# A decoder layer's MLP: three 256-column matmuls per weight tile become one of 512 columns and one of 256

## The chip, the cores and the metric

The kernel runs on one core of a Trainium2 chip. The metric is the device time of one execution in microseconds (us). The time of the kernel before is the median of three runs; one further execution was taken with the hardware profiler, and all rows below come from it.

## What is computed

One decoder layer over 256 tokens of width 2048, all in float32: modulated RMSNorm, an input projection, two kinds of attention, an output projection with a gated residual, then modulated RMSNorm and an MLP, then a last RMSNorm. What the change touches is the MLP (hidden width 8192):

```
h = rmsnorm(x, mlp_norm_g) * (1.0 + sc2) + sh2
u = relu(h @ w_ff1)                  # 2048 -> 8192
x = x + g2 * ((u * u) @ w_ff2)       # 8192 -> 2048
```

`sc2`, `sh2`, `g2` are slices of `silu(c) @ w_mod + b_mod`.

## The kernel before

Activations stand transposed: 128 features on the partitions, the 256 tokens (`S`) as columns. A weight matrix is read from memory in pieces of 1 MB (128 x 2048) into a ring of buffers (`raw`), one DMA each, issued on SyncE's queue (SP).

**Split precision.** A large product isn't run on plain float32 tiles. `split` (L186) makes of each half of a weight piece (128 x 1024) a high part on ScalarE (ACT, L191, rounded to the type float32r) and a low part, the remainder, on VectorE (DVE, L192). Each has three buffers. The activations are split in the same way, into `h2h`/`h2l` and `uh`/`ul`. One tile of weights (128 x 128) times one tile of activations (128 x 256) is then three matmuls of 256 columns into the same 256 columns of a PSUM bank (`mm3`, L195): high weights by high activations (L196), high weights by low activations (L197), low weights by high activations (L198). I call these three a *step*. On the chip a matmul instruction has its own weight load, which the trace shows as the engine PEld beside PE. The matmuls of the stages before (input projection L262, attention) run on plain float32 tiles; the trace shows each of them as two matmuls.

**The MLP.** The hidden width is worked in 8 blocks of 1024, each of 8 tiles of 128. Blocks 0 and 1 are made first, in a loop over the 16 input tiles that holds all 8 PSUM banks (`pf`, L656 to L678). After that comes a loop, L746: `ff1(e)` makes block `e` (e from 2 to 7), `ff2(e - 2)` multiplies an earlier block into the 16 output tiles; `ff2(6)` and `ff2(7)` close.

- `ff1(e)` (L699): for each of 8 tiles `f`, one weight piece, 16 steps into the bank `pu`, then `u_out` (L649): on ACT relu out of PSUM (L651), square (L652), high part (L653); on DVE the low part (L654).
- `ff2(e)` (L716): for each pair of output tiles, one weight piece; for each output tile 8 steps into a bank `pd`, then one instruction that takes the bank's 256 columns: for e = 0 a copy on ACT into `y_sb`, for 1 to 5 an add on DVE (L734), for 6 and 7 a multiply-add into the residual `x_sb` (L739). In block 7 each output tile then goes into the sum of squares of the last RMSNorm.

The part of the modulation that gives `g2` is made during this loop: 16 pieces of `w_mod`, each reduced on DVE (L167), called by `pump_g2` at fixed places. A scheduler turns the program into one fixed order for each engine; every engine works its own list in order.

Earlier in the kernel, in the input projection, pieces of `w_mod` go through a ring of six buffers (`early_ring`, L150): two of the pool `rawp` and the four activation buffers `ah0`, `al0`, `ah1`, `al1`, which later hold the attention's output (`mixh`, `mixl`) and then `h2h`, `h2l`.

Of the kernel before, what the change touches and what calls it, by code (L numbers as in the profile page):

```python
# [46 lines left out]
WM = 3  # L47
G2F = (1, 5)
G2E = (3, 4, 5, 6)
G2E2 = (0, 1, 2, 3)  # L50
G2A = 6
LEADK = (1, 1)
PBN = 8

# [2 lines left out]
def kernel(  # L57
# [86 lines left out]
    def raw(name):  # L144
        return ring("w", name)
# [4 lines left out]
    def early_ring(name):  # L150
        n = early["n"] % 6
        early["n"] += 1
        if n < 2:
            return rawp.tile([P, 2048], F32, tag="rawm", name=name, bufs=NM)
        return actp.tile([P, 2048], F32, tag=("ah0", "al0", "ah1", "al1")[n - 2], name=name)

    def mod_col(part, i):

# [33 lines left out]
        V.tensor_tensor(out=lo, in0=src, in1=hi.bitcast(F32), op=ALU.subtract)  # L192
        return hi, lo

    def mm3(out, wh, wl, ah, al, start, stop, **kw):  # L195
        T.matmul(out, lhsT=wh, rhs=ah, start=start, stop=False, **kw)  # L196
        T.matmul(out, lhsT=wh, rhs=al, start=False, stop=False, **kw)  # L197
        T.matmul(out, lhsT=wl, rhs=ah, start=False, stop=stop, **kw)  # L198


    ap_stack = ExitStack()
# [75 lines left out]
        stage1_mm(kt, hs.pop(kt))  # L277
    nc.sync.dma_start(con, consts)
    g1 = []
    bias = [actp.tile([P, 8, S], F32, tag=f"a{g}1", name=f"bias{g}") for g in "hl"]  # L280
# [5 lines left out]
    mixh = [actp.tile([P, 8, S], F32R, tag="ah0", name="mixh0")]  # L286
# [180 lines left out]
    with tc.high_priority():  # L467
# [94 lines left out]
        units[0].rows()  # L562
        for n, u in enumerate(units):
            if n == 8:
                mixh.append(actp.tile([P, 8, S], F32R, tag="ah1", name="mixh1"))
                mixl.append(actp.tile([P, 8, S], F32R, tag="al1", name="mixl1"))
# [33 lines left out]
    for half in range(2):  # L600
        if half:
            ap_stack.close()
            wide_stack = ExitStack()
            wide.update(pool=wide_stack.enter_context(tc.tile_pool(name="wide", bufs=1)), w=WW, m=WM)
        for dp in range(8):
            w = raw(f"wo{half}_{dp}")
            nc.sync.dma_start(w, w_out[half, dp])
            for d2 in range(2):
                d = 2 * dp + d2
                wh, wl = split(w, d2, f"wo{half}_{dp}")  # L610
                pd = bank(f"pd{half}_{d}")
                for k in range(8):
                    o = k * P
                    mm3(pd[:, 0:S], wh[:, o : o + P], wl[:, o : o + P], mixh[half][:, k, :],
                        mixl[half][:, k, :], k == 0, k == 7)
# [8 lines left out]
        r2 = ss2.rstd()  # L624


    h2h_ = [actp.tile([P, 8, S], F32R, tag=f"ah{i}", name=f"h2h{i}") for i in range(2)]
    h2l_ = [actp.tile([P, 8, S], F32R, tag=f"al{i}", name=f"h2l{i}") for i in range(2)]
    h2h = [h2h_[kt // 8][:, kt % 8, :] for kt in range(KT)]
    h2l = [h2l_[kt // 8][:, kt % 8, :] for kt in range(KT)]  # L630

    def h2_tile(kt):
        a2 = small(f"a2_{kt}")
        V.tensor_tensor(out=a2, in0=sc2[kt], in1=vec[:, V_GM + kt : V_GM + kt + 1], op=ALU.mult)
        xn = tmp.tile([P, S], F32, tag="xn2", name=f"xn2_{kt}")
        if kt < 1:
            V.scalar_tensor_tensor(out=xn, in0=x_sb[:, kt, :], scalar=a2, in1=r2, op0=ALU.mult, op1=ALU.mult)
        else:
            G.tensor_scalar(out=xn, in0=x_sb[:, kt, :], scalar1=a2, scalar2=None, op0=ALU.mult)  # L639
            G.tensor_tensor(out=xn, in0=xn, in1=r2, op=ALU.mult)  # L640
        A.activation(out=h2h[kt], in_=xn, func=AF.Identity, bias=sh2[kt])  # L641
        V.scalar_tensor_tensor(out=h2l[kt], in0=xn, scalar=sh2[kt], in1=h2h[kt].bitcast(F32),
                               op0=ALU.add, op1=ALU.subtract)

    def new_u(e):
        return (up_pool.tile([P, 8, S], F32R, tag="uh", name=f"uh{e}"),
                up_pool.tile([P, 8, S], F32R, tag="ul", name=f"ul{e}"))

    def u_out(u, f, src):  # L649
        r = tmp.tile([P, S], F32, tag="relu", name="relu")  # L650
        A.activation(out=r, in_=src, func=AF.Relu)  # L651
        A.activation(out=r, in_=r, func=AF.Square)  # L652
        A.activation(out=u[0][:, f, :], in_=r, func=AF.Copy)  # L653
        V.tensor_tensor(out=u[1][:, f, :], in0=r, in1=u[0][:, f, :].bitcast(F32), op=ALU.subtract)  # L654

    pf = [bank(f"pf{b}") for b in range(8)]  # L656

# [1 line left out]
    for kt in range(KT):  # L659
# [56 lines left out]
    def ff2(e):  # L716
        uh, ul = us.pop(e)
        for dp in range(8):
            if e in G2E2 and dp in G2F:
                pump_g2(1)  # L720
            w = raw(f"wf2_{e}_{dp}")
            nc.sync.dma_start(w, w_ff2[e, dp])
            for d2 in range(2):
                d = 2 * dp + d2
                wh, wl = split(w, d2, f"wf2_{e}_{dp}")
                pd = bank(f"pd{e}_{d}")
                for k in range(8):
                    o = k * P
                    mm3(pd[:, 0:S], wh[:, o : o + P], wl[:, o : o + P], uh[:, k, :], ul[:, k, :], k == 0, k == 7)

                if e == 0:
                    A.activation(out=y_sb[:, d, :], in_=pd[:, 0:S], func=AF.Copy)
                elif e < G2A:
                    V.tensor_tensor(out=y_sb[:, d, :], in0=pd[:, 0:S], in1=y_sb[:, d, :], op=ALU.add)  # L734
                else:
                    if e == G2A:
                        V.scalar_tensor_tensor(out=x_sb[:, d, :], in0=y_sb[:, d, :], scalar=g2[d],
                                               in1=x_sb[:, d, :], op0=ALU.mult, op1=ALU.add)
                    V.scalar_tensor_tensor(out=x_sb[:, d, :], in0=pd[:, 0:S], scalar=g2[d], in1=x_sb[:, d, :],  # L739
                                           op0=ALU.mult, op1=ALU.add)  # L740
                if e == 7:
                    ss3.add(d)
                    A.activation(out=x_sb[:, d, :], in_=x_sb[:, d, :], func=AF.Copy,
                                 scale=vec[:, V_GF + d : V_GF + d + 1])

    for e in range(2, 8):  # L746
        ff1(e)
        ff2(e - 2)
    for e in (6, 7):
        ff2(e)  # L750
# [38 lines left out]
def _pack(inp):  # L789
# [62 lines left out]
```

## Time and profile before

| | |
|---|---|
| median of 3 runs | 1099.46 us (1096.85 to 1099.94) |
| profiled execution | 1097.01 us, of which the span from first to last instruction is 1095.2 us |
| mean granted TensorE clock | 0.987 of full speed |
| busy share of the span | PE 96%, PEld 90%, DVE 67%, ACT 44%, POOL 11% |
| bytes read | 275 MB, 253 GB/s over the span |
| chain that ended last | PE 84%, DVE 5%, DMA 4%, POOL 3% |

Matmuls overlap in the trace: one of 256 columns is shown as 283 ns long, while the next starts 120 ns after it. What a matmul costs in a stream is therefore read from starts, or from counts in a window, not from its length. In a table by windows the number in brackets counts every instruction that touches the window. SPq is SyncE's queue of DMA issues. A time in brackets at a row's end is idle time of the engine just before it, with what ended it.

### The profile page before, as it was taken

What the parts mean: (1) busy time and instruction counts of PE and PEld (TensorE: products, weight loads), DVE (VectorE), ACT (ScalarE), POOL (GpSimd) and SP (SyncE); (2) the same over time, 40 slices, a digit from 0 to 9 for tenths busy, and PEclk for the clock granted to TensorE, in tenths of its full rate; (3) what the DMA queues carried; (4) which work ended last, traced back from release to release, by engine and by line L of the source; (5) the groups of instructions that cost most, each with busy time, mean ns of one, the idle gap of its engine ahead of it and who ended that gap; (6) DMA issues with size and microseconds to landing.
All of it is one profiled execution on the core that took longest, in us unless ns stands there. A gap on an engine that the chain in (4) does not pass through costs nothing.

```text
span 1095.2 us, 18790 instructions
## 1 busy us (share of the span) xinstructions
PE 1047.9 (96%) x7860; PEld 990.0 (90%) x7860; DVE 733.8 (67%) x948; ACT 482.6 (44%) x788; POOL 115.4 (11%) x88
## 2 busy tenths in 40 slices
PE   5999999999977999999999999999999999999995
PEld 4777756689977999999999999999999999999995
DVE  6776478799986898887755555545554555676554
ACT  2000176643442435764553454355345345533362
POOL 1000012000337453000000000000000000000043
PEclk9999999999998999999999999999999999999997
DMA  8999976689996774888855555555455555554541
GB/s 345 427 427 426 415 277 231 224 313 402 426 426 233 281 280 181 308 338 324 326 209 188 193 180 174 186 193 182 170 188 192 183 171 186 192 185 169 186 155 77
DMA packets 42357, 278.43 MB, mean 254 GB/s; under 512 B 4832, under 2 KB 7456, under 8 KB 11424
## 3 DMA queue, kind: packets, MB, share of 16 engines
q1 hardware_dynamic: 42272, 277.23, 67.0%
q8 instruction: 61, 1.00, 0.4%
q14 instruction: 24, 0.20, 0.0%
HBM read 275.09 MB, written 2.12 MB: 253 GB/s over the span
## 4 chain that ended last, share of the span: by engine, by line
PE 84%; DVE 5%; DMA 4%; POOL 3%; issue 2%; ACT 2%; SPq 0%; DVEq 0%; ACTq 0%; POOLq 0%
PE pd L197 13%; PE pd L196 13%; PE pd L198 13%; PE pu L198 8%; PE pu L196 8%; PE pu L197 8%; PE pj L262 7%; DMA wi<-in_w_in 3%; DVE wm L167 2%; POOL xn L639 2%; PE pf L198 1%; PE pf L196 1%; PE pf L197 1%; DMA wm<-in_w_mod 1%; PE poa L416 1%
## 5 line engine op out<-in xcount | busy, mean ns | idle before, releaser
L192 DVE TENSOR_TENSOR wf_l<-wf,wf_h 128x1024 fp32r<-128x1024 f32 x256 | 314.0, 1229 | 186.2 <-ACT wf_h L191 185.6
L191 ACT ACTIVATE wf_h<-wf 128x1024 fp32r<-128x1024 f32 x256 | 270.1, 1058 | 333.3 <-PE pd L197 206.2
L196 PE MATMUL pd<-uh,wf_h 128*128 128x256 f32 x1024 | 290.2, 283 | 0.0
L197 PE MATMUL pd<-ul,wf_h 128*128 128x256 f32 x1024 | 289.8, 283 | 0.0
L198 PE MATMUL pd<-uh,wf_l 128*128 128x256 f32 x1024 | 289.8, 283 | 0.0
L198 PE MATMUL pu<-h2h,wf_l 128*128 128x256 f32 x768 | 217.4, 283 | 0.0
L196 PE MATMUL pu<-h2h,wf_h 128*128 128x256 f32 x768 | 217.3, 283 | 0.0
L197 PE MATMUL pu<-h2l,wf_h 128*128 128x256 f32 x768 | 217.3, 283 | 0.0
L197 PEld LDWEIGHTS pd<-ul,wf_h 128*128 128x128 f32 x1024 | 196.6, 192 | 0.1
L196 PEld LDWEIGHTS pd<-uh,wf_h 128*128 128x128 f32 x1024 | 196.6, 192 | 0.1
L198 PEld LDWEIGHTS pd<-uh,wf_l 128*128 128x128 f32 x1024 | 196.6, 192 | 0.0
L167 DVE CUSTOM_DVE_ANT_0 wm<-wm,c_bc,vec 128x2048 f32<-128x2048 f32 x64 | 151.7, 2371 | 2.7 <-DMA wm<-in_w_mod 2.6
L198 PEld LDWEIGHTS pu<-h2h,wf_l 128*128 128x128 f32 x768 | 147.4, 192 | 0.2 <-DVE wf_l L192 0.2
L197 PEld LDWEIGHTS pu<-h2l,wf_h 128*128 128x128 f32 x768 | 147.4, 192 | 0.0
L196 PEld LDWEIGHTS pu<-h2h,wf_h 128*128 128x128 f32 x768 | 147.4, 192 | 0.0
L262 PE MATMUL pj<-h,wi 128*128 128x256 f32 (+1 forms) x480 | 111.4, 388 | 9.7 <-ACT h L251 8.1
L262 PEld LDWEIGHTS pj<-h,wi 128*128 128x128 f32 (+1 forms) x480 | 88.0, 189 | 32.9 <-issue 12.8
L589 POOL TENSOR_TENSOR sqa<-sqa,sqr 128x256 f32<-128x256 f32 x26 | 34.5, 1327 | 741.7 <-ACT sqr L587 741.7
L167 DVE CUSTOM_DVE_ANT_0 wm<-wm,c_bc,b 128x2048 f32<-128x2048 f32 x32 | 77.3, 2415 | 26.9 <-DMA wm<-in_w_mod 26.9
L196 PE MATMUL pf<-h2h,wf_h 128*128 128x256 f32 x256 | 72.6, 288 | 8.9 <-ACT h2h L641 7.2
L198 PE MATMUL pf<-h2h,wf_l 128*128 128x256 f32 x256 | 72.1, 288 | 5.0 <-DVE wf_l L192 5.0
L197 PE MATMUL pf<-h2l,wf_h 128*128 128x256 f32 x256 | 72.9, 287 | 0.0
(170 smaller groups left out, 1243.6 us busy)
## 6 DMA issues: line engine op xcount, KB each, us to landing
wm<-in_w_mod SPq DMA_DIRECT2D x96, 1024.0 KB, 7.8
wf<-in_w_ff SPq DMA_DIRECT2D x64, 1024.0 KB, 4.8
wf<-in_w_ff1b SPq DMA_DIRECT2D x48, 1024.0 KB, 4.8
wo<-in_w_out SPq DMA_DIRECT2D x16, 1024.0 KB, 10.1
wf<-in_w_ff1a SPq DMA_DIRECT2D x16, 1024.0 KB, 8.6
wi<-in_w_in SPq DMA_DIRECT2D x15, 928.0 KB, 13.0
x_sb<-in_xT SPq DMA_DIRECT2D x4, 512.0 KB, 5.2
biash<-g_dr SPq DMA_DIRECT2D x1, 1024.0 KB, 12.0
```

Of the source, the lines that this page charges most:

```text
L167: V.tensor_tensor_reduce(out=t, in0=t, in1=c_bc, scale=1.0, scalar=init, op0=ALU.mult, op1=ALU.add, accum_out=col)
L191: A.activation(out=hi, in_=src, func=AF.Copy)
L192: V.tensor_tensor(out=lo, in0=src, in1=hi.bitcast(F32), op=ALU.subtract)
L196: T.matmul(out, lhsT=wh, rhs=ah, start=start, stop=False, **kw)
L197: T.matmul(out, lhsT=wh, rhs=al, start=False, stop=False, **kw)
L198: T.matmul(out, lhsT=wl, rhs=ah, start=False, stop=stop, **kw)
L262: T.matmul(proj(j)[: e - j * P, :], lhsT=w[:, j * P : e], rhs=h, start=(kt == 0 and j % 2 == 0), stop=(kt == KT - 1), skip_group_check=True)
L416: T.matmul(po[64 * g : 64 * g + 64, :], lhsT=vA[:, kb if b else 1, 64 * g : 64 * g + 64], rhs=pt, start=(kb == 0), stop=(kb == len(pts) - 1))
L589: G.tensor_tensor(out=sqa, in0=sqa, in1=sq, op=ALU.add)
L639: G.tensor_scalar(out=xn, in0=x_sb[:, kt, :], scalar1=a2, scalar2=None, op0=ALU.mult)
```

## The change

1. **Matmuls.** In `ff1` for blocks 2 to 7 and in all of `ff2`, a step is now two matmuls (`mm2`): high weights by 512 columns, which are the high and the low activations side by side, into all 512 columns of the bank; then low weights by the 256 columns of the high activations, into the bank's first 256 columns. The bank's two halves are added afterwards. `w_out` and blocks 0 and 1 keep three matmuls.
2. **Layout.** High and low activations share a tile: `h2`, `u` and `mix` are 128 x 8 x 512 in place of two of 128 x 8 x 256. The four early buffers become two of double size, each taken by two successive pieces of `w_mod`.
3. **Adding the halves.** After an `ff1` tile ACT copies the second half out of PSUM and DVE adds the first half to it; `u_out` works on that sum. In `ff2` two instructions take the two halves.
4. **Quarters.** `ff2(q)` sums over two blocks (16 steps into one bank) for each of the 16 output tiles, four times in all; `w_ff2` is packed for that, a piece of 1 MB per output tile. The order becomes ff1(2), ff2(0), ff1(3), ff1(4), ff2(1), ff1(5), ff1(6), ff2(2), ff1(7), ff2(3).

```diff
+        if n % 2 == 0:
+            early["pair"] = actp.tile([P, 2, 2048], F32, tag=f"a{(n - 2) // 2}", name=name)
+        return early["pair"][:, n % 2, :]
...
+    def mm2(out, wh, wl, a, start, stop):
+
+        T.matmul(out, lhsT=wh, rhs=a, start=start, stop=False)
+        T.matmul(out[:, 0:S], lhsT=wl, rhs=a[:, 0:S], start=False, stop=stop)
...
     def new_u(e):
-        return (up_pool.tile([P, 8, S], F32R, tag="uh", name=f"uh{e}"),
-                up_pool.tile([P, 8, S], F32R, tag="ul", name=f"ul{e}"))
+        return up_pool.tile([P, 8, 2 * S], F32R, tag="u", name=f"u{e}")
...
-                mm3(pu[:, 0:S], wh[:, o : o + P], wl[:, o : o + P], h2h[k], h2l[k], k == 0, k == KT - 1)
-            u_out(us[e], f, pu[:, 0:S])
+                mm2(pu, wh[:, o : o + P], wl[:, o : o + P], h2[k], k == 0, k == KT - 1)
+            both = tmp.tile([P, S], F32, tag="part", name=f"both{e}_{f}")
+            A.activation(out=both, in_=pu[:, S : 2 * S], func=AF.Copy)
+            V.tensor_tensor(out=both, in0=pu[:, 0:S], in1=both, op=ALU.add)
+            u_out(us[e], f, both)
...
+    def ff2(q):
+
+        uu = (us.pop(2 * q), us.pop(2 * q + 1))
+        for d in range(KT):
+            if q < 2 and d % 4 == 1:
                 pump_g2(1)
+            w = raw(f"wf2_{q}_{d}")
+            nc.sync.dma_start(w, w_ff2[q, d])
+            pd = bank(f"pd{q}_{d}")
+            for k in range(KT):
+                if k % 8 == 0:
+                    wh, wl = split(w, k // 8, f"wf2_{q}_{d}")
+                o = (k % 8) * P
+                mm2(pd, wh[:, o : o + P], wl[:, o : o + P], uu[k // 8][:, k % 8, :], k == 0, k == KT - 1)
+            y = y_sb[:, d, :]
+            lo, hi = pd[:, S : 2 * S], pd[:, 0:S]
+
+            if q == 0:
+                A.activation(out=y, in_=lo, func=AF.Copy)
+                V.tensor_tensor(out=y, in0=hi, in1=y, op=ALU.add)
+            elif q < 3:
+                V.tensor_tensor(out=y, in0=lo, in1=y, op=ALU.add)
+                V.tensor_tensor(out=y, in0=hi, in1=y, op=ALU.add)
+                if q == 2:
+                    V.scalar_tensor_tensor(out=x_sb[:, d, :], in0=y, scalar=g2[d], in1=x_sb[:, d, :],
                                            op0=ALU.mult, op1=ALU.add)
+            else:
+                for src in (lo, hi):
+                    V.scalar_tensor_tensor(out=x_sb[:, d, :], in0=src, scalar=g2[d], in1=x_sb[:, d, :],
+                                           op0=ALU.mult, op1=ALU.add)
```

**PE, the first two steps of block 3** (`pu3_0` is its first bank, `wf1_3_0_h0` and `_l0` are the high and the low weights of the piece's first half; `h2h0`, `h2l0`, and `h2_0` after the change, are the activations). Before:

```order
L196 MATMUL pu3_0_4809<-h2h0_2575,wf1_3_0_h0_4810 128x256
L197 MATMUL pu3_0_4809<-h2l0_2577,wf1_3_0_h0_4810 128x256
L198 MATMUL pu3_0_4809<-h2h0_2575,wf1_3_0_l0_4811 128x256
L196 MATMUL pu3_0_4809<-h2h0_2575,wf1_3_0_h0_4810 128x256
L197 MATMUL pu3_0_4809<-h2l0_2577,wf1_3_0_h0_4810 128x256
L198 MATMUL pu3_0_4809<-h2h0_2575,wf1_3_0_l0_4811 128x256
```

and now four matmuls for the same two steps (the fifth row begins the third step):

```order
L203 MATMUL pu3_0_4918<-h2_0_2562,wf1_3_0_h0_4919 128x512
L204 MATMUL pu3_0_4918<-h2_0_2562,wf1_3_0_l0_4920 128x256
L203 MATMUL pu3_0_4918<-h2_0_2562,wf1_3_0_h0_4919 128x512
L204 MATMUL pu3_0_4918<-h2_0_2562,wf1_3_0_l0_4920 128x256
L203 MATMUL pu3_0_4918<-h2_0_2562,wf1_3_0_h0_4919 128x512
```

The number of matmuls goes from three to two a step, and nothing comes between them.

**ACT, the end of the first and of the second tile of block 3** (L651 to L653 before are L652 to L654 now; L191 is the high part of a weight piece). Before:

```order
L651 ACTIVATE relu_4866<-pu3_0_4809 128x256
L652 ACTIVATE relu_4866<-relu_4866 128x256
L653 ACTIVATE uh3_4805<-relu_4866 128x256
L191 ACTIVATE wf1_3_2_h1_4970<-wf1_3_2_4939 128x1024
L191 ACTIVATE wf1_3_3_h0_5006<-wf1_3_3_5003 128x1024
L651 ACTIVATE relu_4930<-pu3_1_4873 128x256
```

and now:

```order
L714 ACTIVATE both3_0_4959<-pu3_0_4918 128x256
L652 ACTIVATE relu_4962<-both3_0_4959 128x256
L191 ACTIVATE wf1_3_2_h1_5045<-wf1_3_2_5022 128x1024
L653 ACTIVATE relu_4962<-relu_4962 128x256
L654 ACTIVATE u3_4915<-relu_4962 128x256
L191 ACTIVATE wf1_3_3_h0_5076<-wf1_3_3_5073 128x1024
L714 ACTIVATE both3_1_5010<-pu3_1_4969 128x256
```

The copy L714 is new, and the relu behind it reads `both`, which DVE writes in between; the weight piece `wf1_3_2_h1`, which PE first uses in the middle of the tile after next, stands behind them in either order.

**DVE, block 2, after the change**, around the adds of its fifth and sixth tile (L715 is the new add, L167 with `wm5` a reduction for `g2`, L655 a low part of `u`, L192 the low part of a weight piece):

```order
L192 TENSOR_TENSOR wf1_2_6_l0_4071<-wf1_2_6_4067,wf1_2_6_h0_4070 128x1024
L655 TENSOR_TENSOR u1_3689<-relu_3977,u1_3689 128x256
L715 TENSOR_TENSOR both2_4_3998<-pu2_4_3947,both2_4_3998 128x256
L167 ISA wm5_3_4776,mod5_3_4778<-wm5_3_4776,c_bc_99,vec_78 128x2048
L167 ISA mod5_3_4778 128x1
L655 TENSOR_TENSOR u2_3700<-relu_4001,u2_3700 128x256
L655 TENSOR_TENSOR u1_3689<-relu_4013,u1_3689 128x256
L192 TENSOR_TENSOR wf1_2_6_l1_4096<-wf1_2_6_4067,wf1_2_6_h1_4095 128x1024
L715 TENSOR_TENSOR both2_5_4059<-pu2_5_4008,both2_5_4059 128x256
```

Between the adds stand the same kinds of work as before, one L715 per tile more; six reductions for `g2` fall into this block now as before.

## Rows read from the trace of the kernel before

**Rows 1.** The page: busy time, share of the span and instructions of each engine.

```profile
PE 1047.9 (96%) x7860; PEld 990.0 (90%) x7860; DVE 733.8 (67%) x948; ACT 482.6 (44%) x788; POOL 115.4 (11%) x88
```

**Rows 2.** Who waited for whom, PE from 420 us on: total us, times, longest.

```profile
PE pr L594 <- ACT sqr L587: 1.1, 1, 1.1
PE pf L198 <- DVE wf_l L192: 1.0, 1, 1.0
PE pf L196 <- ACT wf_h L191: 0.9, 1, 0.9
```

**Rows 3.** Windows, PE alone: stretch, length, busy (instructions), granted clock, DMA share, GB/s.

```profile
500.00:1070.00 570.00, 570.00 (x4752) 1.00 0.55 194
327.00:336.00 9.00, 3.94 (x18) 0.50 0.89 332
```

**Rows 4.** Timeline in ff2: start, us, engine, instruction.

```profile
700.22 0.28 PE L198 MATMUL pd<-uh,wf_l 128*128 128x256 f32 x1
700.23 0.19 PEld L196 LDWEIGHTS pd<-uh,wf_h 128*128 128x128 f32 x1
700.34 0.28 PE L196 MATMUL pd<-uh,wf_h 128*128 128x256 f32 x1
```

**Rows 5.** Windows, all engines: PE, PEld, DVE, ACT, POOL, granted clock, DMA.

```profile
434.90:481.20 46.30, 46.30 (x386) 46.11 (x385) 40.42 (x49) 37.24 (x79) 0.00 (x0) 1.00 0.84 321
573.50:945.00 371.50, 371.50 (x3098) 371.50 (x3097) 197.73 (x226) 173.32 (x228) 0.00 (x0) 1.00 0.53 184
```

**Rows 6.** Instructions by line: one of ff1's three matmuls and one of ff2's.

```profile
L196 PE MATMUL pd<-uh,wf_h 128*128 128x256 f32 x1024 | 290.2, 283 | 0.0
L196 PE MATMUL pu<-h2h,wf_h 128*128 128x256 f32 x768 | 217.3, 283 | 0.0
```

**Rows 7.** Timeline, plain float32 matmuls of 128, 256 and 512 columns, runs merged.

```profile
222.36 0.49 PE L455 MATMUL pob<-pTb,vB 128*128 128x128 f32 x2 [0.74 <-ACT pTb L360]
222.36 1.16 PE L455 MATMUL pob<-pTb,vB 128*128 128x128 f32 x8 [0.74 <-ACT pTb L360]
103.67 0.89 PE L262 MATMUL pj<-h,wi 128*128 128x256 f32 x3 [0.21 <-DMA wi<-in_w_in]
103.67 2.61 PE L262 MATMUL pj<-h,wi 128*128 128x256 f32 x11 [0.21 <-DMA wi<-in_w_in]
148.70 1.13 PE L510 MATMUL pvb<-wukv,ckv 128*128 128x512 f32 x2 [0.91 <-DVE ckv L316]
148.70 2.84 PE L510 MATMUL pvb<-wukv,ckv 128*128 128x512 f32 x6 [0.91 <-DVE ckv L316]
```

**Rows 8.** Timeline, steps of blocks 0 and 1 inside the second window of rows 3.

```profile
335.35 0.41 PE L197 MATMUL pf<-h2l,wf_h 128*128 128x256 f32 x1
335.56 0.41 PE L198 MATMUL pf<-h2h,wf_l 128*128 128x256 f32 x1
```

**Rows 9.** Instructions by line: work on a tile that leaves PSUM, and a reduction.

```profile
L651 ACT ACTIVATE relu<-pu 128x256 f32<-128x256 f32 x48 | 17.6, 367 | 0.0
L734 DVE TENSOR_TENSOR y_sb<-pd,y_sb 128x256 f32<-128x256 f32 x80 | 34.0, 425 | 52.7 <-PE pd L198 52.7
L739 DVE SCALAR_TENSOR_TENSOR x_sb<-pd,mod,x_sb 128x256 f32<-128x256 f32 x32 | 15.5, 484 | 26.4 <-PE pd L198 26.4
L167 DVE CUSTOM_DVE_ANT_0 wm<-wm,c_bc,vec 128x2048 f32<-128x2048 f32 x64 | 151.7, 2371 | 2.7 <-DMA wm<-in_w_mod 2.6
```

**Rows 10.** Timeline: ACT, a weight split in block 2.

```profile
441.22 1.06 ACT L191 ACTIVATE wf_h<-wf 128x1024 fp32r<-128x1024 f32 x1 [1.82 <-PE pu L197]
```

**Rows 11.** Timeline at the end: the last matmul of ff2 and what follows it.

```profile
1081.43 0.28 PE L198 MATMUL pd<-uh,wf_l 128*128 128x256 f32 x1
1081.75 0.48 DVE L739 SCALAR_TENSOR_TENSOR x_sb<-pd,mod,x_sb 128x256 f32<-128x256 f32 x1 [3.45 <-PE pd L198]
1082.33 0.42 ACT L587 ACTIVATE sqr<-x_sb 128x256 f32<-128x256 f32 x1 [2.97 <-DVE x_sb L739]
```

**Rows 12.** Timeline in the input projection: DVE on an early piece of `w_mod`.

```profile
41.19 2.35 DVE L167 CUSTOM_DVE_ANT_0 wm<-wm,c_bc,b 128x2048 f32<-128x2048 f32 x1 [1.90 <-DMA wm<-in_w_mod]
```

More of the change, by code (lines that the diff above doesn't have):

```diff
@@ L49 @@
 G2E = (3, 4, 5, 6)
-G2E2 = (0, 1, 2, 3)
-G2A = 6
 LEADK = (1, 1)
@@ L193, in split, with mm3 @@
         return hi, lo
[L195 to L198, printed above, removed]
+    def mm3(out, wh, wl, a, start, stop, **kw):
+        T.matmul(out, lhsT=wh, rhs=a[:, 0:S], start=start, stop=False, **kw)
+        T.matmul(out, lhsT=wh, rhs=a[:, S : 2 * S], start=False, stop=False, **kw)
+        T.matmul(out, lhsT=wl, rhs=a[:, 0:S], start=False, stop=stop, **kw)
+    def mm2(out, wh, wl, a, start, stop):
+        T.matmul(out, lhsT=wh, rhs=a, start=start, stop=False)
+        T.matmul(out[:, 0:S], lhsT=wl, rhs=a[:, 0:S], start=False, stop=stop)
     ap_stack = ExitStack()
@@ L279 @@
     g1 = []
-    bias = [actp.tile([P, 8, S], F32, tag=f"a{g}1", name=f"bias{g}") for g in "hl"]
+    bias_t = actp.tile([P, 16, S], F32, tag="a1", name="bias")
+    bias = [bias_t[:, 8 * g : 8 * g + 8, :] for g in range(2)]
     for g in range(2):
@@ L283 @@
                                            ap=[[1, P], [NG, 8], [1, S]]))
-    mixh = [actp.tile([P, 8, S], F32R, tag="ah0", name="mixh0")]
+    mix = [actp.tile([P, 8, 2 * S], F32R, tag="a0", name="mix0")]
     for d in range(NG1):
@@ L564 @@
             if n == 8:
-                mixh.append(actp.tile([P, 8, S], F32R, tag="ah1", name="mixh1"))
-                mixl.append(actp.tile([P, 8, S], F32R, tag="al1", name="mixl1"))
+                mix.append(actp.tile([P, 8, 2 * S], F32R, tag="a1", name="mix1"))
             u.turn()
@@ L613 @@
                     o = k * P
-                    mm3(pd[:, 0:S], wh[:, o : o + P], wl[:, o : o + P], mixh[half][:, k, :],
-                        mixl[half][:, k, :], k == 0, k == 7)
+                    mm3(pd[:, 0:S], wh[:, o : o + P], wl[:, o : o + P], mix[half][:, k, :], k == 0, k == 7)
                 V.scalar_tensor_tensor(out=x_sb[:, d, :], in0=pd[:, 0:S], scalar=g1[d], in1=x_sb[:, d, :],
@@ L624 @@
         r2 = ss2.rstd()
[L627 to L630, printed above, removed]
+    h2_ = [actp.tile([P, 8, 2 * S], F32R, tag=f"a{i}", name=f"h2_{i}") for i in range(2)]
+    h2 = [h2_[kt // 8][:, kt % 8, :] for kt in range(KT)]
     def h2_tile(kt):
@@ L652, in u_out @@
         A.activation(out=r, in_=r, func=AF.Square)
-        A.activation(out=u[0][:, f, :], in_=r, func=AF.Copy)
-        V.tensor_tensor(out=u[1][:, f, :], in0=r, in1=u[0][:, f, :].bitcast(F32), op=ALU.subtract)
+        A.activation(out=u[:, f, 0:S], in_=r, func=AF.Copy)
+        V.tensor_tensor(out=u[:, f, S : 2 * S], in0=r, in1=u[:, f, 0:S].bitcast(F32), op=ALU.subtract)
     pf = [bank(f"pf{b}") for b in range(8)]
@@ L675 @@
             mm3(pf[j // 2][:, (j % 2) * S : (j % 2) * S + S], wh[:, o : o + P], wl[:, o : o + P],
-                h2h[kt], h2l[kt], kt == 0 and j % 2 == 0, kt == KT - 1, skip_group_check=True)
+                h2[kt], kt == 0 and j % 2 == 0, kt == KT - 1, skip_group_check=True)
         if kt == 0:
@@ L713, in ff1 @@
             if e in G2E and f in G2F:
                 pump_g2(1)
[L716 to L719, printed above, removed]
+    def ff2(q):
+        uu = (us.pop(2 * q), us.pop(2 * q + 1))
+        for d in range(KT):
+            if q < 2 and d % 4 == 1:
                 pump_g2(1)
[L721 to L739, printed above, removed]
-                                           op0=ALU.mult, op1=ALU.add)
[L741 to L750, printed above, removed]
+            w = raw(f"wf2_{q}_{d}")
[7 more added lines that the diff above has]
+            y = y_sb[:, d, :]
@@ new lines, in ff2 @@
+            lo, hi = pd[:, S : 2 * S], pd[:, 0:S]
[7 more added lines that the diff above has]
+                    V.scalar_tensor_tensor(out=x_sb[:, d, :], in0=y, scalar=g2[d], in1=x_sb[:, d, :],
+                                           op0=ALU.mult, op1=ALU.add)
+            else:
+                for src in (lo, hi):
+                    V.scalar_tensor_tensor(out=x_sb[:, d, :], in0=src, scalar=g2[d], in1=x_sb[:, d, :],
+                                           op0=ALU.mult, op1=ALU.add)
+                ss3.add(d)
+                A.activation(out=x_sb[:, d, :], in_=x_sb[:, d, :], func=AF.Copy,
+                             scale=vec[:, V_GF + d : V_GF + d + 1])
@@ L751 @@
+    ff1(2)
+    ff2(0)
+    for q in range(1, 3):
+        ff1(2 * q + 1)
+        ff1(2 * q + 2)
+        ff2(q)
+    ff1(7)
+    ff2(3)
     assert len(g2) == KT
```

12 lines of the change are left out of this document (5 added, 7 removed).

## The prediction, made before the changed kernel ran

> **What bounds the kernel now.** I read first the busy shares, then the waits of PE, then PE's rate in windows, then what the other engines have left in the same windows.
>
> PE and its weight loads are busy nearly all the time, DVE two thirds, ACT less than half [rows 1]. A busy PE alone proves little, so the waits come next: from 420 us to the end PE waits three times, 3.0 us in all [rows 2], two of them in blocks 0 and 1, which keep their matmuls, and one in the last RMSNorm. In blocks 2 to 7 and in ff2 PE waits for nobody. What is left is PE's own rate: 4752 matmuls in 570.00 us at full clock, 120 ns each [rows 3], and single starts show the same, 700.22 and 700.34 [rows 4]. So a step of three costs 360 ns. ff1 makes 768 of them and ff2 1024 [rows 6], together 1792, or 645 us: 59% of the span hangs on this one price. The change is worth what it does to a step, as long as ACT, DVE and the DMAs keep up.
>
> **The step.** Before and after, a step moves 768 columns: three times 256, now 512 and 256. If PE were paid by the column, nothing would be won. So the question is what the 120 ns consist of. Where the granted clock is 0.50, the 1.2 GHz level [rows 3], the same matmuls start 0.21 us apart [rows 8]: 256 columns, one a clock, with nothing on top. At 2.4 GHz 256 columns would be 107 ns. Thus 13 of the 120 ns are not columns; they are covered at half clock and stick out at full clock. Three accounts fit these rows, and they part at 512 columns.
>
> To weigh them I use the plain float32 matmuls of the attention, which also have a weight load each [rows 7]. From the differences of merged runs: 128 columns (1.16 - 0.49) / 6 = 0.112 us, 256 columns (2.61 - 0.89) / 8 = 0.215 us, 512 columns (2.84 - 1.13) / 4 = 0.428 us. They take two clocks a column, so plain 128 fills the array as long as float32r 256, and plain 256 as long as float32r 512. At the shorter of these times plain costs 5 ns over its columns, at the longer 2 ns: what sticks out gets no larger as a matmul gets longer. Against plain at equal array time, float32r pays 120 - 112 = 8 ns more.
>
> *Lower bound* of the 512-column matmul: 215 ns, the plain row of equal array time, if the 8 ns vanish under a longer matmul. *Upper bound*: 2 x 120 = 240 ns, if they come per column. *Taken*: 215 + 8 = 223 ns, the 8 ns once per matmul. I take the middle because the plain rows speak against growth with length, while no row shows a warm float32r matmul without the excess. The matmul of 256 columns stays at 120 ns; its load starts behind a matmul, 0.01 us after that one's start [rows 4], and now has a longer one to hide under for every second load.
>
> A new step is 223 + 120 = 343 ns, 17 ns less (16.7 before rounding). 1792 x 16.7 = **29.9 us less**.
>
> The Trainium skill has a formula for this ("TensorE: Matmul & The Clock Gate", section Back-to-back issue gap): a warm matmul costs its columns over 2.4 plus 2.5 ns. It speaks against this change: by it the step goes from 3 x 109.2 to 215.8 + 109.2 ns, a gain of 2.5 ns, estimated at 4.5 us in all. The trace agrees for plain float32 at 256 columns (0.215), not for the matmul in question (0.120 where it says 0.109).
>
> **Other edits, with what hides each.**
>
> - *Adding the halves in ff1*: 48 copies on ACT at about 0.37 us and 48 adds on DVE at 0.43 us [rows 9], 18 and 20 us. In the window from 573.50 ACT is busy 173 and DVE 198 of 371 us [rows 5], so they fit. ACT now stands a moment for DVE's add, with a weight split behind it. But that split is needed one and a half tiles later, 8 us, and may begin only when PE frees its buffer: ACT waits for PE there, 1.82 us [rows 10]. Cost 0.
> - *Block 2* is the tightest place: blocks 0 and 1 leave PSUM there and six reductions for g2 run on DVE (2.4 us each [rows 9]). DVE is busy 40.4 of 46.3 us, ACT 37.2 [rows 5]. The block's 128 steps shrink it by 2.1 us to 44.2; DVE gets 8 x 0.43 more, 43.8. That is full. Nothing is late as long as the lead in weight splits lasts; I take 0. If the cover goes, DVE is late next: with the 5.9 us that it idled there before, 43.8 + 5.9 = 49.7 us, 5.5 us lost. That is the other end.
> - *ff2*: before, 16 copies on ACT, and on DVE 80 + 32 instructions [rows 9] and 16 multiply-adds for e = 6; now 16 and 128, the same on DVE. Cost 0.
> - *Order and DMAs*: as many pieces of 1 MB, one per 16 steps, now each 5.5 us rather than 5.8. DMA share 0.53 at 184 GB/s in the long window [rows 5] becomes about 193 GB/s; 321 is sustained in block 2. A block of `u` is overwritten only after the ff2 that read it, which stands earlier in PE's order. Cost 0.
> - *Early buffers in pairs*: the first DMA of a pair waits for two reductions instead of one. In the input projection DVE waits for the piece to land, 1.90 us [rows 12]; the buffer's last reader is three input tiles back. SP waits for PE with the `w_in` pieces anyway. Cost 0; at worst one reduction, 2.4 us.
> - *The end*: the last output tile has two multiply-adds after its last matmul instead of one, and Square waits for them [rows 11]: **+0.5 us** (0.48).
>
> **Sum.** 1097.0 (the profiled execution) - 29.9 + 0.5 = 1067.6 us. That execution lies 2.4 us under the median of the runs, so for a median I add 2.4: **1070.0 us**.
>
> **Rivals.** All times are for a median, built like the sum.
>
> 1. *The excess is a floor.* Under a matmul of 215 ns nothing sticks out, as at half clock, where 213 ns of columns cover all of it [rows 8]. Then the step is 335 ns, 1792 x 25 = 44.8 us less: **1055**. For it: the half-clock rows and the plain row of 256 columns. Against: float32r's 8 ns over plain at equal array time. In block 2 DVE would then be a little over PE, with up to 5.5 us back.
> 2. *Columns are paid, the change gives nothing.* If float32r is fed at 0.47 ns a column at full clock (120 / 256), 512 columns cost 240 and the step stays at 360 ns: 1097.0 + 0.5 + 2.4 = **1100**. For it: the 120 ns are steady over 4752 matmuls, and at half clock such a feed would not show. Against: plain 128 shows an excess of the same kind that 256 and 512 lose. A milder form: plain matmuls have 2 ns over their columns at the longer array times, and one matmul less a step could still give that, 1792 x 2 = 3.6 us: 1096. The formula of the Trainium skill quoted above ("TensorE: Matmul & The Clock Gate") is this milder form, with 2.5 ns.
> 3. *Slower: the 512-column matmul is worse than two of 256.* If a feed of 0.47 ns a column is the rule and float32r's 8 ns come on top per long matmul, L203 costs 248 ns, the step 368: 1792 x 8.3 = 14.9 us more, **1115**. It decides from 242 ns on: there 1792 x 2 ns exceed the 3.3 us (0.3%) that a measurement of this kernel can tell from no change. Against: the plain rows, where 512 costs a little under twice 256.
>
> **Chances.** Forecast (512 columns at 219 to 229 ns, 1062 to 1080 us): 0.43. Rival 1: 0.27. Between the forecast and rival 2 (230 to 238 ns, 1082 to 1096): 0.08. Rival 2: 0.17, of which 0.03 is the milder form that still counts as faster. Rival 3, or rival 2 with block 2 late on top: 0.05. Faster by over 0.3%: 0.43 + 0.27 + 0.08 + 0.03 = 0.81. Within 0.3%: 0.17 - 0.03 = 0.14. Slower: 0.05. The range reaches from a little under rival 1 to the cases short of rival 2, 1052 to 1094, and leaves out 0.2: rivals 2 and 3.
>
> **What would show it.** In the new profile I look at PE in ff2: from a start of L203 to the next start of L204, 0.22 us for the forecast, 0.215 for rival 1, 0.24 for rival 2, 0.25 for rival 3; from L204 to L203 0.12. ff1 and ff2 end to end should take 1792 x 0.343 = 615 us, against 645. PE's waits should show nothing new from block 2 on; a wait for a weight split (L191, L192) in block 2 would be the DVE cost that I set to 0. ACT's and DVE's busy times should grow by 18 and 20 us. After the last matmul the end should be 0.5 us longer. I am wrong if PE waits for ACT or DVE in every tile of ff1, or if the matmul of 256 columns, behind a long one, no longer costs 120 ns.

## The result, and the profile after

The changed kernel takes **1087.4 us** (median of 4 executions, 1076.4 to 1088.4) where the kernel before takes 1099.5 beside it; the ratio is 0.988, with a 95% interval of 0.984 to 0.991. That is 1.2% faster; the forecast was 2.7%. The prediction's range, 1052 to 1094, holds the time, and the direction is right, but the gain is 12 us and not 29.

The median hides something that the rest can't be understood without: executions of this one kernel come in two groups. With three more runs of it, unaltered (below), there are 16 executions: 6 lie between 1076.0 and 1079.4 us, 10 between 1085.3 and 1089.3, none between. The profile after is of the lower group: 1076.42 us, span 1074.6, mean granted clock 0.985. So the median depends on how many executions of a run fell into which group.

The page of the changed kernel, busy time and share of each engine, which answers to [rows 1], and the instructions of the MLP by line, which answer to [rows 6] (one line of before is one of three such matmuls, here L203 is the matmul of 512 columns and L204 that of 256):

```profile
PE 1025.7 (95%) x6068; PEld 893.2 (83%) x6068; DVE 744.3 (69%) x996; ACT 493.4 (46%) x836; POOL 112.0 (10%) x88
...
L203 PE MATMUL pd<-u,wf_h 128*128 128x512 f32 x1024 | 357.0, 393 | 0.0
L204 PE MATMUL pd<-u,wf_l 128*128 128x256 f32 x1024 | 286.9, 280 | 0.0
L203 PE MATMUL pu<-h,wf_h 128*128 128x512 f32 x768 | 266.5, 391 | 0.0
```

PE is as full as before, with 1792 matmuls fewer: 7860 - 6068. So the first question is again whether anybody keeps it waiting. Who waited for whom, PE from 420 us to the end (total us, times, longest), which answers to [rows 2]:

```profile
PE pr L599 <- ACT sqr L592: 1.6, 1, 1.6
PE pf L199 <- DVE wf_l L192: 1.0, 1, 1.0
PE pf L197 <- ACT wf_h L191: 0.9, 1, 0.9
```

The same three waits, in the same places; the first of them, in the last RMSNorm, is 0.5 us longer, the longer end that was forecast. The difference to the forecast is not in a wait; it is in PE's own rate. The timeline in ff2 (start, us, engine, instruction), which answers to [rows 4]:

```profile
700.07 0.39 PE L203 MATMUL pd<-u,wf_h 128*128 128x512 f32 x1
700.30 0.28 PE L204 MATMUL pd<-u,wf_l 128*128 128x256 f32 x1
700.42 0.39 PE L203 MATMUL pd<-u,wf_h 128*128 128x512 f32 x1
700.65 0.28 PE L204 MATMUL pd<-u,wf_l 128*128 128x256 f32 x1
700.76 0.39 PE L203 MATMUL pd<-u,wf_h 128*128 128x512 f32 x1
```

From L203 to L204 it is 0.23 us, from L204 to L203 0.12 or a little under. Two starts of L203 lie 0.35 and 0.34 apart; over long stretches the step is 346.7 ns. That is not the whole kernel, though. Windows of PE alone (stretch, length, busy and instructions, granted clock, DMA share, GB/s), which answer to [rows 3]:

```profile
450.00:960.00 510.00, 510.00 (x2944) 1.00 0.60 218
990.00:1050.00 60.00, 60.00 (x342) 1.00 0.44 158
```

Divide each length by half its count: 346.5 ns a step in the long stretch, 351 in the short one (an instruction that overlaps an edge counts too; by single starts the steps of the short one are 353.3 ns on average). Clock 1.00 in both, no wait in either, the same two instructions. The rate changes at this place:

```profile
974.28 0.39 PE L203 MATMUL pd<-u,wf_h 128*128 128x512 f32 x1
974.51 0.28 PE L204 MATMUL pd<-u,wf_l 128*128 128x256 f32 x1
974.63 0.73 PE L203 MATMUL pd<-u,wf_h 128*128 128x512 f32 x2
974.86 0.19 PEld L203 LDWEIGHTS pd<-u,wf_h 128*128 128x128 f32 x1 [0.16 <-DVE u L655]
975.20 0.40 PE L204 MATMUL pd<-u,wf_l 128*128 128x256 f32 x2
```

The first tile of the last ff2 call reaches block 7 of `u`, whose last low part DVE (L655) has just written, and a weight load waits 0.16 us for it. At the same place PE's fixed order leaves its pattern, once in the whole stream: two matmuls of 512 columns in a row (x2), then two of 256. From there to the matmuls of the last RMSNorm that come in between near 1054 us, a step costs 6.7 ns more on average than before.

The whole account of this execution against the one before: the first matmul of block 2 starts at 436.34 instead of 435.15 us (+1.2); from there to the last matmul of ff2, at 1060.36, it is 624.0 us instead of 646.3 (-22.3), 348.2 ns per step on average instead of 360.7; and from that matmul to the end of the span 14.3 us instead of 13.8 (+0.5). Together -20.6, as 1097.0 to 1076.4.

### The profile page after: what moved, and what is told of

Same layout as the page of the kernel before. It is cut to its first block, busy times and chain, and to the rows that moved or that the text cites. A ratio compares the mean times of both kernels' runs of the same rounds, so it can differ in the third digit from the quotient of the medians.

```text
span 1074.6 us, 15326 instructions
## 1 busy us (share of the span) xinstructions
PE 1025.7 (95%) x6068; PEld 893.2 (83%) x6068; DVE 744.3 (69%) x996; ACT 493.4 (46%) x836; POOL 112.0 (10%) x88
## 4 chain that ended last, share of the span: by engine, by line
PE 85%; DVE 5%; POOL 3%; DMA 3%; issue 2%; ACT 2%; SPq 1%; DVEq 0%; ACTq 0%; POOLq 0%
PE pd L203 22%; PE pu L203 16%; PE pd L204 11%; PE pj L268 9%; PE pu L204 9%; PE pd L198 2%; PE pd L197 2%; PE pd L199 2%; POOL xn L641 2%; DVE wm L167 2%; PE pf L199 1%; PE pf L197 1%; PE pf L198 1%; DMA wi<-in_w_in 1%; DMA wm<-in_w_mod 1%
## 5 line engine op out<-in xcount | busy, mean ns | idle before, releaser
L192 DVE TENSOR_TENSOR wf_l<-wf,wf_h 128x1024 fp32r<-128x1024 f32 x256 | 313.6, 1227 | 199.0 <-ACT wf_h L191 196.1
L191 ACT ACTIVATE wf_h<-wf 128x1024 fp32r<-128x1024 f32 x256 | 269.9, 1057 | 242.9 <-PE pd L203 177.7
L203 PE MATMUL pd<-u,wf_h 128*128 128x512 f32 x1024 | 357.0, 393 | 0.0
L204 PE MATMUL pd<-u,wf_l 128*128 128x256 f32 x1024 | 286.9, 280 | 0.0
L203 PE MATMUL pu<-h,wf_h 128*128 128x512 f32 x768 | 266.5, 391 | 0.0
L203 PEld LDWEIGHTS pd<-u,wf_h 128*128 128x128 f32 x1024 | 191.7, 187 | 43.3 <-DVE u L655 0.2
L204 PE MATMUL pu<-h,wf_l 128*128 128x256 f32 x768 | 215.1, 280 | 0.0
L204 PEld LDWEIGHTS pd<-u,wf_l 128*128 128x128 f32 x1024 | 193.5, 189 | 0.1
L203 PEld LDWEIGHTS pu<-h,wf_h 128*128 128x128 f32 x768 | 143.6, 187 | 31.4
L167 DVE CUSTOM_DVE_ANT_0 wm<-wm,c_bc,vec 128x2048 f32<-128x2048 f32 x64 | 151.7, 2370 | 1.6 <-DMA wm<-in_w_mod 1.6
L204 PEld LDWEIGHTS pu<-h,wf_l 128*128 128x128 f32 x768 | 145.2, 189 | 0.3 <-DVE wf_l L192 0.3
L167 DVE CUSTOM_DVE_ANT_0 wm<-wm,c_bc,b 128x2048 f32<-128x2048 f32 x32 | 77.3, 2414 | 28.4 <-DMA wm<-in_w_mod 28.4
L197 PE MATMUL pf<-h,wf_h 128*128 128x256 f32 x256 | 73.2, 290 | 8.6 <-ACT h L643 7.2
L198 PE MATMUL pf<-h,wf_h 128*128 128x256 f32 x256 | 73.1, 288 | 0.0
L197 PE MATMUL pd<-mix,wo_h 128*128 128x256 f32 x256 | 72.9, 285 | 0.0
L198 PE MATMUL pd<-mix,wo_h 128*128 128x256 f32 x256 | 72.4, 283 | 0.0
```

The costliest lines, as they stand in the source:

```text
L167: V.tensor_tensor_reduce(out=t, in0=t, in1=c_bc, scale=1.0, scalar=init, op0=ALU.mult, op1=ALU.add, accum_out=col)
L197: T.matmul(out, lhsT=wh, rhs=a[:, 0:S], start=start, stop=False, **kw)
L198: T.matmul(out, lhsT=wh, rhs=a[:, S : 2 * S], start=False, stop=False, **kw)
L203: T.matmul(out, lhsT=wh, rhs=a, start=start, stop=False)
L204: T.matmul(out[:, 0:S], lhsT=wl, rhs=a[:, 0:S], start=False, stop=stop)
```

## The experiments

**The changed kernel again** (no edit), to see what its own scatter is made of.

> The changed kernel itself, run again. Its profiled execution took 1076.4 us, three others 1086.4 to 1088.4. Theory A: a step has two steady prices, 346.7 ns and 353.3 ns (both stand in the first trace, the second from 975 us on, behind a PE wait), and the long executions ran at the second one from block 2 on: 1554 steps x 6.6 ns = 10.3 us. Then each new execution lies near 1076 or near 1087, and the new trace, whichever it is, has all its steps at one of the two prices between its PE waits. Theory B: the long executions wait somewhere (DVE full in block 2, a late DMA): then times spread between 1076 and 1088 and a long one shows PE waits from block 2 on that add up to 10 us.

1087.4 us (1086.1 to 1089.3, 4 executions), ratio 0.990 (0.988 to 0.992). The profiled execution took 1086.1 us, and its windows of PE, set against those above, are the other way round:

```profile
450.00:960.00 510.00, 510.00 (x2889) 1.00 0.59 215
990.00:1050.00 60.00, 60.00 (x348) 1.00 0.53 189
```

510 us by half of 2889 is 353.1 ns: here the long stretch runs at the slower step, and the quicker one comes only after the place where the order leaves its pattern, at 986 us. Its timeline at 700 us, as shown above, and at that place:

```profile
700.04 0.40 PE L203 MATMUL pd<-u,wf_h 128*128 128x512 f32 x1
700.27 0.28 PE L204 MATMUL pd<-u,wf_l 128*128 128x256 f32 x1
700.39 0.40 PE L203 MATMUL pd<-u,wf_h 128*128 128x512 f32 x1
700.63 0.28 PE L204 MATMUL pd<-u,wf_l 128*128 128x256 f32 x1
700.75 0.40 PE L203 MATMUL pd<-u,wf_h 128*128 128x512 f32 x1
...
985.77 0.28 PE L204 MATMUL pd<-u,wf_l 128*128 128x256 f32 x1
985.89 0.62 PE L203 MATMUL pd<-u,wf_h 128*128 128x512 f32 x2
986.35 0.40 PE L204 MATMUL pd<-u,wf_l 128*128 128x256 f32 x2
```

0.35, then 0.36. At 985.89 the two long matmuls take 0.46 us together: here PE does not stand still, and the rate changes all the same. From the first matmul of block 2 (437.27) to the last of ff2 (1070.03) it is 632.76 us, against 624.02 in the profile after: 8.7 of the 9.7 us between these two executions are there, PE's waits are the same three, and the granted clock is 1.00 in both. So one stream of alternating lengths has **two steady phases**, 346.7 and 353.3 ns a step, and the time of an execution hangs on which of them its long stretch fell into. (Four of the 16 executions were profiled. The three of the lower group have the quicker step in the long stretch, the one of the upper group has the slower; for the other twelve the phase is inferred from the time.)

**Three matmuls of 256 columns, everything else as changed** (order of operands, `u` as one tile, the adding of halves, the pairs):

```
-        T.matmul(out, lhsT=wh, rhs=a, start=start, stop=False)
-        T.matmul(out[:, 0:S], lhsT=wl, rhs=a[:, 0:S], start=False, stop=stop)
+        T.matmul(out[:, 0:S], lhsT=wh, rhs=a[:, 0:S], ...)
+        T.matmul(out[:, S : 2 * S], lhsT=wh, rhs=a[:, S : 2 * S], ...)
+        T.matmul(out[:, 0:S], lhsT=wl, rhs=a[:, 0:S], ...)
```

> The new order, layout and evacuation, but the 512-column matmul is two of 256 into the two halves of the bank. If the gain is the matmul's alone, a step is 360 ns again and the time is that of the kernel before plus about 0.5 us for the end: 1097 to 1100 us, ratio 1.000 to 1.002. If the other edits cost something (block 2, pairs of buffers, quarters), it is above that by that much; if they gain, below.

1099.8 us (1098.4 to 1101.0, 10 executions), ratio 1.0011 (1.0000 to 1.0022). Its PE waits are the three of before, its step 360.0 ns, and from the first matmul of block 2 (437.63) to the last of ff2 (1084.18) it takes 646.5 us, against 646.3. All other edits together cost some 1 us (0 to 2.4 by the interval) and win nothing; what the change gives, the long matmul gives.

**Both weights on 512 columns.**

```
-        T.matmul(out[:, 0:S], lhsT=wl, rhs=a[:, 0:S], start=False, stop=stop)
+        T.matmul(out, lhsT=wl, rhs=a, start=False, stop=stop)
```

> The low weights multiply 512 columns too (this adds the product of both low parts), so PE runs one kind of matmul only, 1792 x 2 of 512 columns. It measures the disputed price alone. Excess once per matmul, 13.3 ns: 226.7 ns each, step 453 ns. Excess vanishing: 215.8 each, step 432. Per column: 240 each, step 480. Times 1076 + 1792 x (step - 347): 1266, 1228, 1314 us.

1269.0 us, a single execution. Starts in ff1, and a window of PE:

```profile
699.70 0.39 PE L204 MATMUL pu<-h,wf_l 128*128 128x512 f32 x1
699.93 0.39 PE L203 MATMUL pu<-h,wf_h 128*128 128x512 f32 x1
700.16 0.39 PE L204 MATMUL pu<-h,wf_l 128*128 128x512 f32 x1
700.38 0.39 PE L203 MATMUL pu<-h,wf_h 128*128 128x512 f32 x1
700.61 0.39 PE L204 MATMUL pu<-h,wf_l 128*128 128x512 f32 x1
...
450.00:1230.00 780.00, 780.00 (x3443) 1.00 0.46 165
```

780 us by 3443 is 226.5 ns a matmul; single starts give 226.7, and no second phase. By the half-clock rows [rows 8] a column is one clock, so 512 columns at 2.4 GHz are 213.3 ns: 13.3 ns stick out, as many as with 256 columns (120.0 - 106.7). The excess comes **once per matmul**. It does not vanish under a long matmul (215 ns, rival 1), and it is not paid per column (240 ns, rivals 2 and 3). Every matmul of these kernels has its own weight load, so no run here can tell whether the excess belongs to the matmul or to its load.

**The short matmul first** (L203 and L204 change places, nothing else).

> The 256-column matmul with the low weights comes ahead of the 512-column one. The columns and the loads are the same. Theory A (price by the two matmuls, two steady phases): steps at 346.7 or 353.3 ns again, times near 1076 or 1087. If instead it matters which weights are loaded under the long matmul, the step changes by some ns: 1792 x 5 ns is 9 us.

1088.1 us (1084.5 to 1091.8, 4 executions), ratio 0.989 (0.986 to 0.992). The profiled execution took 1091.8 us: its block 2 began at 441.70 us, 5.4 later than in the profile after, which is lost before the first matmul that this edit touches, and its steps took 353.3 ns (2889 instructions from 450 to 960 us, as in the first repeat above). So the slower rate is the same in either order within a step. The times miss the expectation in part, since two lie above 1090; none lies in the lower group, but four executions are too few to say that this order draws the quicker phase less often.

**512 columns in ff1 alone**, ff2 with three of 256:

```
-                mm2(pd, wh[:, o : o + P], wl[:, o : o + P], uu[k // 8][:, k % 8, :], k == 0, k == KT - 1)
+                mm3b(pd, wh[:, o : o + P], wl[:, o : o + P], uu[k // 8][:, k % 8, :], k == 0, k == KT - 1)
```

> The 512-column matmul in ff1 alone (768 steps); ff2 has three of 256 into the two halves of the bank (1024 steps). If a step's gain is the matmul's, ff2 is at 360 ns a step and ff1 at 346.7 or 353.3: 10.2 or 5.1 us less than the run with three of 256 everywhere (1099.8), 1089.6 to 1094.7. ff1 and ff2 alternate, so it shows too whether the phase of the mixed stream is set anew after each uniform stretch (different prices in different blocks of ff1 without a PE wait) or only by a wait of PE (one price in all blocks).

1092.5 us (1091.1 to 1094.5, 4 executions), ratio 0.995 (0.993 to 0.996). This run shows when the phase is drawn, since ff1 and ff2 alternate. Windows of PE in three stretches of ff1 and, second from the top, in a call of ff2:

```profile
441.00:480.00 39.00, 39.00 (x227) 1.00 0.83 317
481.00:571.00 90.00, 90.00 (x752) 1.00 0.82 306
573.00:662.00 89.00, 89.00 (x506) 1.00 0.53 190
756.00:843.00 87.00, 87.00 (x504) 1.00 0.55 194
```

ff2 is back at 360.0 ns a step. By single starts the ff1 stretch from 441 to 480 has 346.7 ns, that from 573 to 662 353.3, that from 756 to 843 346.7, and the last one, from 937, 353.3. PE waited for nothing between them. So it takes no wait to change the phase: an even stretch of 256 columns ends it, and the next alternating stretch draws anew.

**Lengths in groups.** If alternating is what the phase needs, runs of equal lengths should be rid of it. Three versions, which issue the products with the low weights after every second, after every eighth and after all sixteen of the 512-column matmuls of an output tile (the last one, in ff2; ff1 likewise):

```
+            lows = []
             for k in range(KT):
...
-                mm2(pd, wh[:, o : o + P], wl[:, o : o + P], uu[k // 8][:, k % 8, :], k == 0, k == KT - 1)
+                lows.append(wl[:, o : o + P])
+                T.matmul(pd, lhsT=wh[:, o : o + P], rhs=uu[k // 8][:, k % 8, :], start=k == 0, stop=False)
+            for k in range(KT):
+                T.matmul(pd[:, 0:S], lhsT=lows[k], rhs=uu[k // 8][:, k % 8, :][:, 0:S], start=False, stop=k == KT - 1)
```

> The same matmuls in the order two of 512, two of 256: half as many changes of length. Theory A': if the slow price is paid per alternation, two steps cost 693.3 ns in the fast phase and at most 700 in the slow one (not 706.7): times 1076 or at most 1082. Rival: as long as lengths are mixed closely, the slow phase costs 6.7 ns a step: near 1087.

Pairs: 1079.3 us (1077.5 to 1081.7, 4 executions), ratio 0.982 (0.980 to 0.984); two steps take 696.7 ns together, 348.3 each.

> The same matmuls as in the changed kernel, but per half of a weight piece first the eight of 512 columns, then the eight of 256: two changes of length per 16 matmuls instead of sixteen. Theory A': a matmul costs its columns plus 13.3 ns (uniform streams: 120.0 and 226.7 ns), and the second steady price, 353.3 ns a step, comes from alternating the two lengths. Then a half takes 8 x (226.7 + 120.0) = 2773 ns plus at most 7 ns, in every execution, and the time is 1074 to 1078 us with no second group near 1087. Rival: the slower price belongs to the 512-column matmul with the chip or the execution, whatever stands beside it; then the time is near 1087 as before.

Eights: 1079.7 us (1078.4 to 1081.8, 4 executions), ratio 0.983 (0.981 to 0.984); 349.1 ns a step. Here the expectation missed: sixteen matmuls of a half took 2793 ns, 20 over 8 x (226.7 + 120) = 2773 and not 7. Within a group some starts of 512 columns lie 236 ns apart, so long matmuls have an irregular spacing near a change of length also.

> Sixteen matmuls of 512 columns, then sixteen of 256: two changes of length per output tile instead of four. In the run with groups of eight a tile cost 16 x 349.15 ns, 39 ns more than 16 x 346.67. If that surplus is paid per change of length, half of it goes: 348 ns a step, 1792 x 1.2 = 2 us less than there, near 1077.5. Rival: the surplus belongs to every 512-column matmul that isn't in an endless uniform stream (its starts scattered between 226 and 236 ns): then nothing changes, near 1079.5. Weight splits are held longer; if PE waits for them, it is slower.

Sixteens: 1076.9 us (1076.0 to 1080.8, 5 executions), ratio 0.981 (0.978 to 0.983), 347.9 ns a step.

**The comparison on one chip.** The run of the changed kernel beside the sixteens happened to give two executions, both of the lower group, where I had expected the upper:

> The changed kernel once more, for a third trace. If the phase of the mixed stream is drawn anew at each PE wait, the stretch from block 2 to ff2(3) stands at 346.7 or at 353.3 ns a step throughout and the short stretch behind the wait in ff2(3) at either; seven of eight executions so far took 1086 to 1089 us, so I expect 353.3.

1075.97 and 1078.64 us, ratio 0.980 (0.977 to 0.983). Thus low times could have belonged to that chip. Both kernels were run once more side by side, on another one.

> The changed kernel once more, unaltered, in the same call as grouped16_b. If a steady phase is drawn in each execution, some of these executions lie at 1076 to 1079 us and some at 1086 to 1089, and the median lies in whichever group has more. If the phase belongs to the chip that a call runs on (the call of again gave 1086 to 1089 four times, that of again_b 1076 and 1079), all executions lie in one group.

> The same kernel as grouped16. Theory: 16 matmuls of 512 columns and then 16 of 256 leave no pair of lengths to alternate, a step costs about 348 ns whatever the phase, so all executions lie at 1076 to 1081 us again, also if the changed kernel beside it draws 1086 to 1089. Rival: the low times of grouped16 belonged to the chip of that call, as those of again_b did; then executions near 1086 to 1089 show up here too, as they do in the run beside it.

Changed kernel: 1076.8, 1086.8, 1078.0, 1085.3, 1087.6, 1079.4 us, ratio 0.985 (0.982 to 0.988). Sixteens: 1076.7 to 1080.9 in 5 executions, ratio 0.982 (0.980 to 0.983). On one chip, in one run, the changed kernel falls into either group, three times each, so the phase is drawn per execution. The sixteens, now 10 executions on two chips, lie between 1076.0 and 1080.9 us; of all three grouped versions, 18 executions, none is over 1081.8, where the upper group begins at 1085.3. Their windows of PE (first run):

```profile
450.00:960.00 510.00, 510.00 (x2937) 1.00 0.60 218
990.00:1050.00 60.00, 60.00 (x348) 1.00 0.47 171
```

Half of 2937 in 510 us is 347.3 ns and half of 348 in 60 us 344.8, alike within what the edges of the windows count. This is the best version found: within what these runs can tell as quick as the changed kernel in its better phase (624.7 us from the first matmul of block 2 to the last of ff2, against 624.0), and no execution was seen in the worse one. Where the changed kernel draws the better one no difference shows, so the two intervals of the last run overlap; the gain is the 9 us of the other executions.

## Why the prediction was right and wrong

**The term that was mis-sized** is the 512-column matmul: "215 + 8 = 223 ns, the 8 ns once per matmul", and with it "A new step is 223 + 120 = 343 ns ... 1792 x 16.7 = 29.9 us less". That the price comes once per matmul was right. Its size was not: I took float32r's 8 ns over plain float32 of equal array time and let the rest shrink as plain float32's does. Measured alone, 512 columns cost 226.7 ns, 213.3 for the columns and the full 13.3 that I had read off the 256-column rows in the same part. From that alone a step is 226.7 + 120 = 346.7, and 1792 x 13.3 = 23.9 us are won, not 29.9: 1076.0 by my own sum, where the lower group lies (1076.0 to 1079.4).

**The assumption beneath it** also fell, and for the median it weighs more: that a step costs the sum of its two matmuls. "The matmul of 256 columns stays at 120 ns", whose failure I had named as a sign of being wrong, does not hold behind a long one: the stretch after a start of L204 is 116.7 ns in the better phase and 116.9 on average in the worse. After L203 it is 230.0 ns in the better phase, which makes the same 346.7 together, and 236.4 on average in the worse. The sign that I had put down, 0.22 us from L203 to L204, thus reads 0.23 also where the step is what the two prices give. So in the worse phase 6.7 ns are added to the sum of the two, the step is 353.3, and 1792 x 6.7 = 11.9 us are won: 1088.0, which is the upper group. Of the 18.0 us from the forecast of 1070.0 to there, the price of the long matmul makes 6.0 and the worse phase 12.0. None of my accounts had a case for that, since no row that I read showed lengths that alternate. The median fell where I had put "between the forecast and rival 2" and a chance of 0.08; the lower group lies inside the forecast's own 1062 to 1080. That the median came from the upper group is the draw: the repeat of two executions beside the sixteens has 1077.3.

**The rivals.** Rival 1, the floor, asked for 215 ns, rival 2 for 240 and rival 3 for 248; at 226.7 ns all three are refuted. The milder form of rival 2, 2 ns a step, is too: even in the worse phase a step gains 6.7. The formula of the Trainium skill ("TensorE: Matmul & The Clock Gate", section Back-to-back issue gap), columns over 2.4 plus 2.5 ns, which that section gives for a matmul by itself, gives an estimate of 215.8 ns for 512 columns; the trace has 226.7, so for float32r it is the addend that differs, 13.3 for 2.5. Its shape, a fixed addend per matmul, is what was measured.

**What hid the other edits** held. ff1's copies and adds, block 2, the reordered DMAs: PE's waits are unchanged but for the 0.5 us at the end, and the kernel with three short matmuls costs some 1 us over the one before. Block 2, which I had called full at 43.8 of 44.2 us of DVE, and the long window that follows (PE, PEld, DVE, ACT, POOL, granted clock, DMA share, GB/s), in the profile after, answer to [rows 5]:

```profile
436.20:480.80 44.60, 44.60 (x258) 39.12 (x257) 40.82 (x55) 38.46 (x86) 0.00 (x0) 1.00 0.86 330
560.00:960.00 400.00, 400.00 (x2310) 352.69 (x2309) 236.90 (x304) 201.75 (x296) 0.00 (x0) 1.00 0.54 190
```

DVE is busy 40.8 of 44.6 us, with 3.8 us to spare, and 5.5 us lost there did not come. At its first step one weight load waits 0.3 us for DVE (L192), where one waited 0.2 before; nothing else of the DVE cost that I had set to 0 showed. The new work by line:

```profile
L714 ACT ACTIVATE both<-pu 128x256 f32<-128x256 f32 x48 | 17.5, 364 | 0.0
L715 DVE TENSOR_TENSOR both<-pu,both 128x256 f32<-128x256 f32 x48 | 20.0, 417 | 0.0
```

17.5 and 20.0 us, as priced. But ACT's busy time grew by 10.8 us (482.6 to 493.4) and DVE's by 10.5 (733.8 to 744.3): busy time counts an overlap of two neighbouring instructions once. Summed over all lines, ACT has 527.8 us where it had 508.8, and DVE 785.3 where it had 766.8, +19.0 and +18.5, near the price; the overlaps take the rest. Block 2 was less full than my sum had it in part for the same reason, since I added durations to a busy time, and in part because five of the six reductions fall into this window now, 2.2 us less of DVE's work.

**The end** came as put down, +0.5 us (from the start of the last matmul to Square 1.42 us instead of 0.90): the two multiply-adds of L748 stand in one row now, 1.00 us where one took 0.48 [rows 11].

```profile
1060.36 0.28 PE L204 MATMUL pd<-u,wf_l 128*128 128x256 f32 x1
...
1060.68 1.00 DVE L748 SCALAR_TENSOR_TENSOR x_sb<-pd,mod,x_sb 128x256 f32<-128x256 f32 x2 [5.59 <-PE pd L204]
1061.78 0.42 ACT L592 ACTIVATE sqr<-x_sb 128x256 f32<-128x256 f32 x1 [5.64 <-DVE x_sb L748]
```

## What to carry to other kernels

Where PE never waits, price a change of shape by the interval between two starts, and take the excess over the columns from the same kind of matmul: here 13.3 ns for a float32r matmul of 256 or of 512 columns in an even stream at granted clock 1.00, so that 512 columns in one are 13.3 ns cheaper than in two. Issue equal lengths in runs rather than in turn; in runs of sixteen it cost 0.7 us here against the better phase, and no execution was 9 us slower any more. And when executions of one kernel fall into two groups with nothing between, profile one of each before explaining a median.

## What the runs showed that I had not expected

A stream of 512- and 256-column float32r matmuls in turn, each with its weight load, at granted clock 1.00 and with nothing waited for, runs at either 346.7 or 353.3 ns a step and keeps its rate for some 1550 steps. Both are means of steady patterns. By single starts the slower one repeats itself every three steps: 233 + 117, 241 + 120 and 236 + 113 ns. The quicker one is 230 + 117 in every step; only behind 986.6 us in the first repeat it comes as steps of 343 and 350 ns with the same mean. Even streams (256 alone at 120.0 ns, 512 alone at 226.7) showed one rate each.

In the traces of alternating steps every change of rate stands at a break in the order of lengths. In the four profiled executions of the changed kernel it is the place near 974 to 986 us with two long matmuls and two short ones in a row, which switched the rate each time, three times to the slower one and once to the quicker. In three of them a weight load also waits 0.16 us there and two starts lie 0.34 us apart; in the one that turned quicker no two starts there lie over 0.24 us apart. The run with the short matmul first has no such place and kept 353.3 ns from block 2 on, until a matmul of the last RMSNorm came in between at 1069.31 us; the three steps behind it took 346.7, and behind the next such matmul, at 1071.13, the slower rate came back. In ff1 alone it is the even stretch of 256 columns. So breaking the order can change the rate without a wait, and no trace has a wait alone that did.

What decides the phase at the start of a stretch was not found out, nor which part of PE holds it. The runs show only that the difference is not time spent waiting, that the granted clock is 1.00 at both rates, that one chip has both, and that the slower rate is the same in either order within a step.
